# Graph attention on one core: a block's third gather ahead of its sums, a fourth load buffer, constants on GpSimd, x loaded later

## The chip, the core and the metric

The kernel runs on one core of one Trainium2 chip. The core has TensorE (PE in the profile; its weight loads stand apart as PEld), VectorE (DVE), ScalarE (ACT), GpSimd (POOL) and SyncE (SP), which run side by side, each through its own list of instructions in order, and wait for each other by semaphores. DMAs are issued from the queues of SP, ACT and POOL (SPq, ACTq, POOLq in the profile). The metric is the device time of one execution in microseconds (us), the median of the runs.

## What is computed

4096 nodes with 64 features, 50000 edges, 4 heads. Cut to what matters:

```python
x_proj[h] = x @ weight[h]
edge_scores[h] = leaky(sum(x_proj[h, src] * att_src[h]) + sum(x_proj[h, dst] * att_dst[h]))
for h in range(n_heads):
    for i in range(num_edges):
        output[h, dst[i]] += np.exp(edge_scores[h, i]) * x_proj[h, src[i]]
# and each output row is divided by the sum of its exps
```

`leaky` multiplies negative scores by 0.2. Edges come in any order; the sum over the edges of a destination is what costs.

## The kernel before, in words

**Sorting (two stages).** Every edge becomes one number that holds its source and destination. Stage 1 sorts 128 rows of 391 edges by source with compare-and-swap passes on DVE (class `Sorter`; `flip`, `half` and others, lines 187 to 252), while ACT counts with sign passes how many keys lie below each bound (`below`, line 263). The sorted rows go to memory (`store`, line 255), are fetched again by source group (`fetch`, line 306), and stage 2 sorts them by destination. Before stage 1, DVE and POOL build small constants (lines 81 to 159): signs per partition (`sj`, `sig`), offsets (`goff`, `off1`, `off2`, `boff`), bounds (`nb1`, `nb2`), partition numbers (`pF`) and selection masks (`m16`, `m8`, `sel1`, `sel2`). Stage 1 can start when the edges `eS` and `eD` have come from memory (lines 72 and 78).

**Tables.** Beside stage 1, PE and ACT make tables from `x` and `weight` (`tables`, lines 321 to 362): `xa` (features and source scores of each node, bf16) and `adb` (an identity and destination scores). `x` is 1 MB in `xf`; it and the weights `wS` are loaded by SP, directly behind the edges. PE's count for stage 1's bounds (`cnt_ps`, line 274) stands behind the tables in PE's list, and DVE reads it when stage 1 is sorted (line 276).

**Blocks.** The destinations are cut in 33 blocks of 125 (`ND`), the edges of a block in 16 groups of 128 (`NT`). For block b:

- `load(b)` (line 410, SP): 1 MB of source and destination numbers, spread to all partitions, into a buffer `bc`.
- `onehot(b)` (lines 438 and 439, DVE): three one-hot matrices `oh` for every group.
- `gather(b, c)` (lines 456 to 464), in three chunks c of 6, 6 and 4 groups: PE multiplies one-hots with the tables into a PSUM tile `ps` (two of these exist), ACT takes exponentials from it (`ex`, line 462) and copies it to `xs` (line 464). The next chunk but one needs that copy, since it uses the same `ps`.
- `weigh(b)` (lines 472 and 477, DVE): weights `wv` from `ex` of all three chunks, then `val` = weights times features from `xs` of all three chunks.
- `sums(b, k)` (lines 488 to 496, PE): k = -1 sums the weights, k = 0 and k = 1 multiply `val` with one-hots into the accumulator `acc`. After k = 1 ACT copies `acc` to `aT` (line 538).
- `project(b)` (line 542, PE) and, for every second block, `give` (lines 547 to 553: DVE divides into `res`, SP writes two blocks to the output).

The order on each engine is written out by hand in `run` (lines 502 to 524), which stands in the printed code below; each engine follows it in order. In the loop's body for block b, PE has: first chunk of b+1, project(b-1), sums(b,-1), second chunk of b+1, sums(b,0), third chunk of b+1, sums(b,1). DVE has weigh(b), onehot(b+2), and for even b the division. SP has the load, then for even b two output writes, which wait for DVE's division; a load also waits until the buffer that it fills has been read by `onehot`.

**Start of the block stage** (lines 614 to 622): POOL fetches windows of sorted edges, DVE unpacks them (`unpack`, lines 379 to 385), SP writes them to `gat_bins` (line 387), from which the loads read. Block 0 is spread on chip instead (`spread`).

The second version of the block stage, under `tc.If` at the end of the file, is for inputs with longer runs and isn't taken here.

Of the kernel before, what the change touches and what calls it, by code (L numbers as in the profile page):

```python
# [11 lines left out]
P = 128  # L12
# [4 lines left out]
OP = mybir.AluOpType  # L17
# [7 lines left out]
RL = RUN * L  # L25
W1 = 256
W2 = 128
BD = 125
# [9 lines left out]
def kernel(ctx: ExitStack, tc: tile.TileContext, x: bass.AP, edge_index: bass.AP,  # L38
                         weight: bass.AP, att_src: bass.AP, att_dst: bass.AP, out: bass.AP):
    nc = tc.nc  # L40
    V, S, G, T = nc.vector, nc.scalar, nc.gpsimd, nc.tensor
    N, Din = x.shape
# [3 lines left out]
    ND = -(-N // BD)  # L46
    NI = -(-ND // 8)
    SG = N // NR
# [32 lines left out]
    pidx = cst.tile([P, 1], I32)  # L81
# [6 lines left out]
    def bits(name, shift, mask):  # L88
        i = cst.tile([P, 1], I32, name=f"{name}_i")
        f = cst.tile([P, 1], F32, name=f"{name}_f")  # L90
        V.tensor_scalar(out=i[:], in0=pidx[:], scalar1=shift, scalar2=mask, op0=OP.logical_shift_right,
                        op1=OP.bitwise_and)
        V.tensor_copy(out=f[:], in_=i[:])
        return f


    sj = []
    for j in range(3):
        f = bits(f"b{j}", j, 1)
        V.tensor_scalar(out=f[:], in0=f[:], scalar1=-2.0, scalar2=1.0, op0=OP.mult, op1=OP.add)  # L100
        sj.append(f)
    sig = cst.tile([P, 1], F32)
    V.tensor_tensor(out=sig[:], in0=sj[0][:], in1=sj[1][:], op=OP.mult)
    V.tensor_tensor(out=sig[:], in0=sig[:], in1=sj[2][:], op=OP.mult)
    ioF = cst.tile([P, P], F32)
    V.tensor_copy(out=ioF[:], in_=io[:])
    nb1 = cst.tile([P, NR + 1], F32)
# [1 line left out]
    p8 = bits("p8", 3, 15)  # L109
# [11 lines left out]
    for i in range(3):  # L121
# [1 line left out]
        G.memset(eps[32 * i:32 * i + 1, :], float(term))  # L123
        left = left - term.astype(np.float32)
    goff = cst.tile([P, 1], F32)
    V.tensor_scalar(out=goff[:], in0=p8[:], scalar1=-float(SG * N), scalar2=None, op0=OP.mult)
    nb2 = cst.tile([P, ND + 1], F32)
    V.tensor_scalar(out=nb2[:], in0=ioF[:, 0:ND + 1], scalar1=-float(BD * SG), scalar2=-float(N * SG), op0=OP.mult,
                    op1=OP.max)
    V.tensor_scalar(out=nb2[:], in0=nb2[:], scalar1=0.5, scalar2=None, op0=OP.add)  # L130
    pF = cst.tile([P, 2], F32)
    V.tensor_copy(out=pF[:, 0:1], in_=pidx[:])
    V.tensor_scalar(out=pF[:, 1:2], in0=pF[:, 0:1], scalar1=float(P), scalar2=None, op0=OP.add)
    off1 = cst.tile([P, 2], F32)
    for i in range(2):
        V.tensor_scalar(out=off1[:, i:i + 1], in0=pm8[:], scalar1=float(RL), scalar2=float(8 * i * RL),
                        op0=OP.mult, op1=OP.add)
    off2 = cst.tile([P, 1], F32)
    V.tensor_scalar(out=off2[:], in0=pm16[:], scalar1=float(RL), scalar2=None, op0=OP.mult)
    boff = cst.tile([P, NI], F32)  # L140
    for i in range(NI):
        V.tensor_scalar(out=boff[:, i:i + 1], in0=p16[:], scalar1=-float(BD * SG), scalar2=-float(8 * i * BD * SG),
                        op0=OP.mult, op1=OP.add)
    m16 = cst.tile([P, 16], F32)
    G.tensor_scalar(out=m16[:], in0=ioF[:, 0:16], scalar1=p8[:, 0:1], scalar2=None, op0=OP.is_equal)
# [175 lines left out]
    def tables(pr, pps, pp1):  # L321

        S.copy(out=identb[:], in_=ident[:])
        xf = pr.tile([P, NB, Din], F32)
        nc.sync.dma_start(out=xf[:], in_=x.rearrange("(b p) d -> p b d", p=P))
        wS = pr.tile([Din, H, Dout], F32)
        nc.sync.dma_start(out=wS[:], in_=weight.rearrange("h c o -> c h o"))
        attbd = pr.tile([P, 2, 4], F32)
        G.memset(attbd[:], 0.0)
        for h in range(H):  # L330
            for k, a in enumerate((att_src, att_dst)):
                nc.gpsimd.dma_start(out=attbd[(h % 2) * 64:(h % 2) * 64 + 64, h // 2, 2 * k + h % 2:2 * k + h % 2 + 1],
                                    in_=a[h:h + 1, :].rearrange("a o -> o a"))
        G.memset(Wbd[:], 0.0)
        for h in range(H):
            hh = h % 2
            nc.gpsimd.dma_start(out=Wbd[hh * 64:hh * 64 + 64, h // 2, hh * 64:hh * 64 + 64], in_=weight[h, :, :])
        uv = pr.tile([Din, 2, H], F32)
        for i in range(2):
            ps = pps.tile([P, Din], F32, tag="pp")  # L340
            T.transpose(out=ps[:], in_=wS[:, 2 * i:2 * i + 2, :], identity=ident[0:Din, 0:Din])
            wT = pr.tile([P, Din], F32, name=f"wT{i}")
            S.copy(out=wT[:], in_=ps[:])
            ps2 = pps.tile([Din, 4], F32, tag="pp")
            T.matmul(out=ps2[:], lhsT=wT[:], rhs=attbd[:, i, :], start=True, stop=True)
            S.copy(out=uv[:, :, 2 * i:2 * i + 2], in_=av(ps2[:], 0, [2, 2], [1, 2]))
        S.copy(out=xa[:, :, 2 * H:XC], in_=xf[:])
        xT = pr.tile([Din, ND * BD + P - BD], F32)
        G.memset(xT[:, N:], 0.0)
        for q in range(NB // 4):  # L350
            ps = pps.tile([Din, 4, P], F32, tag="pp")
            for i in range(4):
                T.transpose(out=ps[:, i, :], in_=xf[:, 4 * q + i, :], identity=ident[:])
            S.copy(out=xT[:, 4 * q * P:4 * (q + 1) * P], in_=ps[:])
        for k, (n, step, to) in enumerate(((NB, P, xa[:, :, 0:2 * H]), (ND, BD, adb[:, :, P:AB]))):
            ps = pp1.tile([P, n, H], F32, name=f"at_ps{k}")
            for b in range(n):
                T.matmul(out=ps[:, b, :], lhsT=xT[:, b * step:b * step + P], rhs=uv[:, k, :], start=(b == 0), stop=True,  # L358
                         skip_group_check=True)
            S.copy(out=to[:, :, 0:H], in_=ps[:])  # L360
            S.mul(out=to[:, :, H:2 * H], in_=ps[:], mul=ALPHA)
        S.copy(out=adb[:, :, 0:P], in_=av(identb[:], 0, [0, ND], [1, P]))
# [32 lines left out]
    class Blocks:  # L395


        def __init__(self, ctx, sink):
            pool = lambda **kw: ctx.enter_context(tc.tile_pool(**kw))
            self.bcp = pool(name="bc", bufs=3)  # L400
            self.bp = pool(name="blk", bufs=2)
            self.psx = pool(name="ps_x", bufs=2, space=PSUM)
            self.psa = pool(name="ps_a", bufs=1, space=PSUM)
            self.sink = sink
            self.bc, self.oh, self.ex, self.xs, self.wv, self.val = ({} for _ in range(6))
# [96 lines left out]
        def run(self, also={}):  # L502
            for c in range(len(CH)):
                self.gather(0, c, V.tensor_copy if c == 1 else S.copy)
            self.onehot(1)
            for b in range(ND):
                self.load(b + 3)
                self.weigh(b, 2 if b == ND - 1 else 1)
                self.gather(b + 1, 0)
                self.onehot(b + 2)  # L510
                if b:
                    self.sink.project(b - 1)
                    if b % 2 == 0:
                        self.sink.give(b - 2, 2)
                self.sums(b, -1)
                self.gather(b + 1, 1)
                self.sums(b, 0)
                self.gather(b + 1, 2)
                self.sums(b, 1)
                if b in also:  # L520
                    also[b]()
            self.sink.project(ND - 1)
            n = 2 - ND % 2
            self.sink.give(ND - n, n)
# [89 lines left out]
    with ExitStack() as st:  # L614
        blocks = Blocks(st, Finish(st))
        win.unpack(0, nc.sync, nc.scalar)
        for b in range(1, 3):
            blocks.load(b)
        for i in range(1, 4):
            win.unpack(i, nc.sync, nc.sync)  # L620
        blocks.spread(0, win.tb[:, 0])
        blocks.run({i - 3: lambda i=i: win.unpack(i, nc.sync, nc.sync) for i in range(4, NI)})
# [3 lines left out]
    with tc.If((n1 > W1) | (n2 > W2)):  # L626
        with tc.tile_pool(name="all", bufs=1) as al:
            total = al.tile([P, ND, AW], F32)
            V.memset(total[:], 0.0)
            with tc.For_i(0, n1, W1):  # L630
                at1 = advance(al, ws1, we1, W1, 1)
                with tc.tile_pool(name="sort3", bufs=1) as so3, tc.tile_pool(name="pp3", bufs=1, space=PSUM) as pp3:
                    group(so3, pp3, at1[:])
                    longest(so3, pp3, ws2, we2, 1)
                m2 = room(1, L)
                with tc.For_i(0, m2, W2):
                    with ExitStack() as st:
                        win = Windows(st.enter_context(tc.tile_pool(name="win", bufs=1)), advance(al, ws2, we2, W2, 2)[:])
                        for i in range(NI):
                            win.unpack(i, nc.sync, nc.scalar)  # L640
                        blocks = Blocks(st, Total(total))
                        for b in range(3):
                            blocks.load(b)
                        blocks.onehot(0)
                        blocks.run()
# [39 lines left out]
```

## Time and profile before

| | us |
|---|---|
| median of 3 runs (lowest, highest) | 319.4 (318.13, 319.46) |
| the profiled execution | 319.96 |
| its span, first to last instruction | 318.1 |
| busy in the span: PE, DVE, ACT, POOL | 209.2, 273.6, 180.6, 19.0 |

The span is cut as follows by the places where an engine takes up the next stage: stage 1 from 5.79 to 70.83 us, stage 2 from 79.10 to 117.04, the block loop's steady part from 141.59 (block 1's `val`) to 301.98 (block 31's `val`). Shares of busy time over the whole span are averages over these stages; what a change in the loop can bring is read in the loop. A timeline row gives the start and the length of an instruction, and in brackets how long its engine stood idle before it and what ended that. Neighbouring instructions on one engine may overlap by some hundredths of a us.

### The profile page before, as it was taken

How to read it: one execution, taken by the hardware profiler on the slowest of the kernel's cores; microseconds unless marked ns; L12 is line 12 of the kernel's file. 1: busy time of each engine (PE TensorE's matmuls, PEld its weight loads, DVE VectorE, ACT ScalarE, POOL GpSimd, SP SyncE). 2: the span in 40 equal slices, each digit the busy share in tenths (PEclk: the TensorE clock that was granted, in tenths of full speed). 3: DMA queues.
4: the chain of work that ended last, by engine and by line, in shares of the span. 5: the costliest groups of instructions: out<-in, count | busy, mean ns of one | idle time of the engine just before them, and what ended most of it. 6: DMA issues, size and time to landing. Idle time of an engine off the chain costs nothing. (4 is left out here: it accounts for less than half of the span.)

```text
span 318.1 us, 8412 instructions
## 1 busy us (share of the span) xinstructions
PE 209.2 (66%) x3534; PEld 193.3 (61%) x3534; DVE 273.6 (86%) x519; ACT 180.6 (57%) x351; POOL 19.0 (6%) x46
## 2 busy tenths in 40 slices
PE   0039999000000008499999989999999999999981
PEld 0027999000000003398989888988888889888970
DVE  7999999993999986889998899899978998899860
ACT  2984001300999400557768767767767677777740
POOL 6800000002000005000000000000000000000000
PEclk9999555555555555979999999999999999999997
DMA  7200000002000002963844865586458556755312
GB/s 201 50 1 0 2 0 0 1 0 66 1 0 0 1 33 51 302 255 102 293 165 193 285 225 163 217 292 223 163 220 279 183 179 258 279 181 187 118 36 55
DMA packets 13070, 41.80 MB, mean 131 GB/s; under 512 B 3088, under 2 KB 8272, under 8 KB 8928
## 3 DMA queue, kind: packets, MB, share of 16 engines
q1 hardware_dynamic: 11944, 40.09, 36.4%
q0 software_dynamic: 704, 0.66, 0.9%
q8 instruction: 30, 0.49, 0.6%
q10 hardware_dynamic: 376, 0.43, 0.4%
q14 instruction: 16, 0.13, 0.1%
HBM read 36.13 MB, written 5.05 MB: 129 GB/s over the span
## 5 line engine op out<-in xcount | busy, mean ns | idle before, releaser
L464 ACT CAST xs<-ps 128x1200 bf16<-128x1200 f32 (+1 forms) x98 | 102.0, 1041 | 0.0
L477 DVE TENSOR_TENSOR val<-xs,wv 128x4096 bf16<-128x4096 bf16 (+1 forms) x34 | 75.7, 2229 | 9.6 <-ACT xs L464 7.8
L496 PE MATMUL acc<-xs,val 128*128 128x125 bf16 x1056 | 70.0, 220 | 9.9 <-DVE val L477 9.0
L456 PE MATMUL ps<-xa,oh 128*128 128x72 bf16 x528 | 73.9, 197 | 3.6 <-DVE oh L438 2.9
L460 PE MATMUL ps<-adb,oh 128*128 128x136 bf16 x528 | 76.0, 225 | 0.0
L458 PE MATMUL ps<-xa,oh 128*128 128x72 bf16 x528 | 73.4, 198 | 1.3 <-DVE oh L439 1.1
L496 PEld LDWEIGHTS <-val 128*128 128x128 bf16 x1056 | 60.5, 99 | 14.8 <-DVE val L477 14.8
L456 PEld LDWEIGHTS <-oh 128*128 128x128 bf16 x528 | 52.2, 99 | 3.5 <-DVE oh L438 3.5
L462 ACT ACTIVATE ex<-ps 128x96 bf16<-128x96 f32 (+1 forms) x99 | 24.2, 245 | 52.1 <-PE ps L460 51.8
L458 PEld LDWEIGHTS <-oh 128*128 128x128 bf16 x528 | 51.9, 98 | 2.9 <-DVE oh L439 2.6
L460 PEld LDWEIGHTS <-oh 128*128 128x128 bf16 x528 | 52.0, 98 | 0.0
L438 DVE TENSOR_SCALAR oh<-bc,pF 128x4096 bf16<-128x4096 bf16 (+2 forms) x35 | 42.8, 1222 | 6.5 <-DMA bc<-gat_bins 5.8
L201 DVE TENSOR_TENSOR sA<-sB 128x256 f32<-128x256 f32 (+2 forms) x108 | 39.7, 409 | 1.9
L201 DVE TENSOR_TENSOR sB<-sA 128x256 f32<-128x256 f32 (+2 forms) x100 | 36.8, 409 | 1.7
L263 ACT ACTIVATE junk<-kr,nb 128x512 f32<-128x512 f32 x33 | 23.8, 722 | 21.9 <-DVE kr L314 20.9
L274 PE MATMUL cnt_ps<-sgn,sel 128*128 128x17 f32 (+1 forms) x6 | 1.7, 390 | 52.2 <-ACT sgn L266 52.2
L274 PEld LDWEIGHTS cnt_ps<-sgn,sel 128*128 128x128 f32 x6 | 1.4, 318 | 52.3 <-issue 52.3
L358 PEld LDWEIGHTS at_ps<-uv,xT 64*128 64x128 f32 x130 | 25.7, 307 | 0.2 <-issue 0.2
L358 PE MATMUL at_ps<-uv,xT 64*128 64x4 f32 x130 | 25.8, 335 | 0.0
L439 DVE TENSOR_SCALAR oh<-bc,pF 128x2048 bf16<-128x2048 bf16 (+2 forms) x35 | 25.1, 717 | 0.0
L542 PE MATMUL pf<-Wbd,aT 128*125 128x128 f32 x132 | 21.9, 288 | 1.7 <-ACT aT L538 0.9
L542 PEld LDWEIGHTS pf<-Wbd,aT 128*125 128x125 f32 x132 | 17.0, 187 | 3.8 <-issue 1.9
(125 smaller groups left out, 200.6 us busy)
## 6 DMA issues: line engine op xcount, KB each, us to landing
bc<-gat_bins SPq DMA_DIRECT2D x32, 1024.0 KB, 9.1
out_dram<-res SPq DMA_DIRECT2D x32, 125.0 KB
gat_sorted<-sA SPq DMA_DIRECT2D x2, 256.0 KB
eS<-in_edge_index_dram SPq DMA_DIRECT2D x1, 390.0 KB
eD<-in_edge_index_dram ACTq DMA_DIRECT2D x1, 390.0 KB
gat_bins<-tb SPq DMA_DIRECT2D x9, 32.0 KB
out_dram<-res SPq DMA_DIRECT2D x1, 96.0 KB, 3.5
win<-gat_sorted,wi POOLq DMA_INDIRECT x5, 2.6
```

Of the source, the lines that this page charges most:

```text
L201: V.tensor_tensor(out=av(d[:], o, [2 * h, n], [1, h]), in0=av(s[:], 0, [2 * h, n], [1, h]), in1=av(s[:], h, [2 * h, n], [1, h]), op=op)
L358: T.matmul(out=ps[:, b, :], lhsT=xT[:, b * step:b * step + P], rhs=uv[:, k, :], start=(b == 0), stop=True, skip_group_check=True)
L438: V.tensor_scalar(out=oh[:, 0:2, e], in0=bc[:, :, e], scalar1=pF[:, 0:1], scalar2=None, op0=OP.is_equal)
L439: V.tensor_scalar(out=oh[:, 2, e], in0=bc[:, 1, e], scalar1=pF[:, 1:2], scalar2=None, op0=OP.is_equal)
L456: T.matmul(out=ps[:, i, P:P + XC], lhsT=oh[:, 1, e], rhs=xa[:, 2 * t, :], start=(i % 2 == 0), stop=False, skip_group_check=True)
L458: T.matmul(out=ps[:, i, P:P + XC], lhsT=oh[:, 2, e], rhs=xa[:, 2 * t + 1, :], start=False, stop=False, skip_group_check=True)
L460: T.matmul(out=ps[:, i, 0:S0], lhsT=oh[:, 0, e], rhs=adb[:, b, :], start=False, stop=True, skip_group_check=True)
L462: S.activation(out=av(ex[:], 2 * t0, [2, n], [2 * NT, 2 * H], [1, 2]), in_=av(ps[:], P, [PW, n], [1, 2 * H], [0, 2]), func=ACTF.Exp)
L464: copy(out=xs[:, t0:t0 + n, 0:P + XC], in_=ps[:, 0:n, 0:P + XC])
L477: V.tensor_tensor(out=av(val[:], h * Dout, [Dout, n], [C, NT], [1, Din]), in0=av(xs[:], S0, [0, n], [XW, NT], [1, Din]), in1=av(wv[:], h * ...
L496: T.matmul(out=self.acc[:, k * BD:(k + 1) * BD], lhsT=val[:, t, k * P:(k + 1) * P], rhs=xs[:, t, 0:BD], start=False, stop=(t == NT - 1), s ...
L542: T.matmul(out=self.pf[0:BD, b % 2, k * P:(k + 1) * P], lhsT=self.aT[:, b % 2, k * BD:(k + 1) * BD], rhs=Wbd[:, k, :], start=(b % 2 == 0 a ...
```

## The change

It has five parts. In `run`, the third chunk of block b+1 stands ahead of `sums(b, 0)` instead of behind it. The pool of `bc` has four buffers instead of three, and loads are issued one block earlier (b+4 in place of b+3, three in place of two before the loop). 25 small constant operations go from DVE to POOL. `x` and `weight` are loaded from ACT's queue; in ACT's list that stands behind the 16 sign passes of stage 1. In the version that isn't taken, loads are one more as well. The diff, with constants of the same kind left out:

```diff
         V.tensor_scalar(out=i[:], in0=pidx[:], scalar1=shift, scalar2=mask, op0=OP.logical_shift_right,
                         op1=OP.bitwise_and)
-        V.tensor_copy(out=f[:], in_=i[:])
+        G.tensor_copy(out=f[:], in_=i[:])
...
-        V.tensor_scalar(out=f[:], in0=f[:], scalar1=-2.0, scalar2=1.0, op0=OP.mult, op1=OP.add)
+        G.tensor_scalar(out=f[:], in0=f[:], scalar1=-2.0, scalar2=1.0, op0=OP.mult, op1=OP.add)
...
-    V.tensor_tensor(out=sig[:], in0=sig[:], in1=sj[2][:], op=OP.mult)
+    G.tensor_tensor(out=sig[:], in0=sig[:], in1=sj[2][:], op=OP.mult)
...
-        V.tensor_scalar(out=boff[:, i:i + 1], in0=p16[:], scalar1=-float(BD * SG), scalar2=-float(8 * i * BD * SG),
+        G.tensor_scalar(out=boff[:, i:i + 1], in0=p16[:], scalar1=-float(BD * SG), scalar2=-float(8 * i * BD * SG),
                         op0=OP.mult, op1=OP.add)
...
-        nc.sync.dma_start(out=xf[:], in_=x.rearrange("(b p) d -> p b d", p=P))
+        nc.scalar.dma_start(out=xf[:], in_=x.rearrange("(b p) d -> p b d", p=P))
         wS = pr.tile([Din, H, Dout], F32)
-        nc.sync.dma_start(out=wS[:], in_=weight.rearrange("h c o -> c h o"))
+        nc.scalar.dma_start(out=wS[:], in_=weight.rearrange("h c o -> c h o"))
...
-            self.bcp = pool(name="bc", bufs=3)
+            self.bcp = pool(name="bc", bufs=4)
...
-                self.load(b + 3)
+                self.load(b + 4)
...
                 self.gather(b + 1, 1)
+                self.gather(b + 1, 2)
                 self.sums(b, 0)
-                self.gather(b + 1, 2)
                 self.sums(b, 1)
...
-        for b in range(1, 3):
+        for b in range(1, 4):
             blocks.load(b)
```

How it stands on PE in the loop's body for block 1, before (`ps_1211` is block 2's second chunk, `ps_1248` its third; `acc_1193` and `val_1157` are block 1's; rows of a chunk or a sum that read alike are left out):

```order
L488 MATMUL acc_1193<-eps_115,one_116 128x4
L491 MATMUL acc_1193<-wv_1155,xs_1033 128x4
...
L460 MATMUL ps_1211<-adb_158,oh_1055 128x136
L496 MATMUL acc_1193<-xs_1033,val_1157 128x125
...
L456 MATMUL ps_1248<-xa_157,oh_1055 128x72
L460 MATMUL ps_1248<-adb_158,oh_1055 128x136
```

And after (the tiles' numbers are two higher up to the second chunk; the third is `ps_1234`):

```order
L488 MATMUL acc_1195<-eps_115,one_116 128x4
L491 MATMUL acc_1195<-wv_1157,xs_1035 128x4
...
L460 MATMUL ps_1213<-adb_158,oh_1057 128x136
...
L460 MATMUL ps_1234<-adb_158,oh_1057 128x136
L496 MATMUL acc_1195<-xs_1035,val_1159 128x125
```

The third chunk has moved from behind the first sixteen matmuls on `val` to in front of them; both sums of `val` now stand together.

SP's list from the program's start into the loop, as a difference:

```order
 L78 DMA eS<-in_edge_index_dram 80x2
-L325 DMA xf<-in_x_dram 128x32x64
-L327 DMA wS<-in_weight_dram 64x4x64
 L255 DMA gat_sorted<-sA 128x512 x2
 L297 TENSOR_LOAD most x2
 L387 DMA gat_bins<-tb 8x16x128
-L410 DMA bc<-gat_bins 128x4096 x2
+L410 DMA bc<-gat_bins 128x4096 x3
 L387 DMA gat_bins<-tb 8x16x128 x6
```

The loads of x and the weights have left SP, and a third load stands ahead of the six writes of unpacked windows; behind that the pattern of two output writes and two loads is the same as before, with each load for the block after the one that it was for.

POOL's list at the program's start, as a difference:

```order
 masks.py:199 AFFINE_SELECT ident<-ident 128x128
+L93 CAST b_f<-b_i 128x1
+L100 TENSOR_SCALAR b_f<-b_f 128x1
...
+L103 TENSOR_TENSOR sig<-b_f 128x1
+L104 TENSOR_TENSOR sig<-sig,b_f 128x1
...
+L126 TENSOR_SCALAR goff<-p_f 128x1
+L128 TENSOR_SCALAR nb_126<-ioF 128x34
...
+L142 TENSOR_SCALAR boff<-p_f 128x1 x5
 L145 TENSOR_SCALAR m_143<-ioF,p_f 128x16
```

The constants that left DVE now stand in POOL's list ahead of the masks, so that the masks, POOL's DMAs for the attention weights and `Wbd` come later.

## Rows read from the trace of the kernel before

**Rows 1.** Stretches: start:end, length; PE, PEld, DVE, ACT, POOL busy; clock; DMA.

```profile
5.79:70.83 65.04, 34.74 (x172) 31.94 (x172) 62.05 (x167) 24.66 (x52) 8.38 (x20) 0.69 0.07 15
141.59:301.98 160.39, 149.58 (x3046) 142.19 (x3043) 143.97 (x155) 115.82 (x212) 0.00 (x0) 1.00 0.59 208
```

**Rows 2.** Waits, loop from 141.59 to 301.98: total us, times, longest.

```profile
PE acc L496 <- DVE val L477: 8.4, 15, 0.6
DVE val L477 <- ACT xs L464: 7.3, 15, 0.5
DVE oh L438 <- DMA bc<-gat_bins: 5.8, 14, 0.9
```

**Rows 3.** DVE's timeline, a pair of blocks: start, length, line, [idle before <-releaser].

```profile
206.00 2.29 DVE L477 TENSOR_TENSOR val<-xs,wv 128x4096 bf16<-128x4096 bf16 x1
208.21 1.28 DVE L438 TENSOR_SCALAR oh<-bc,pF 128x4096 bf16<-128x4096 bf16 x1
...
210.19 0.23 DVE L472 TENSOR_TENSOR wv<-ex 128x128 bf16<-128x128 bf16 x1
210.91 2.29 DVE L477 TENSOR_TENSOR val<-xs,wv 128x4096 bf16<-128x4096 bf16 x1 [0.49 <-ACT xs L464]
213.44 1.28 DVE L438 TENSOR_SCALAR oh<-bc,pF 128x4096 bf16<-128x4096 bf16 x1 [0.24 <-DMA bc<-gat_bins]
...
215.59 0.69 DVE L549 TENSOR_TENSOR res<-pf,inv 125x512 f32<-125x512 f32 x1
...
216.51 2.29 DVE L477 TENSOR_TENSOR val<-xs,wv 128x4096 bf16<-128x4096 bf16 x1
```

**Rows 4.** PE's timeline, same pair.

```profile
208.34 1.05 PE L496 MATMUL acc<-xs,val 128*128 128x125 bf16 x16 [0.57 <-DVE val L477]
...
212.97 0.22 PE L460 MATMUL ps<-adb,oh 128*128 128x136 bf16 x1
```

**Rows 5.** ACT's timeline, same pair: copies of the first and the third chunk.

```profile
206.00 1.15 ACT L464 CAST xs<-ps 128x1200 bf16<-128x1200 f32 x1
...
210.05 0.82 ACT L464 CAST xs<-ps 128x800 bf16<-128x800 f32 x1
```

**Rows 6.** SP's timeline, same pair, and issues by line (KB each, median us to landing).

```profile
206.51 0.83 SPq L410 DMA_DIRECT2D bc<-gat_bins  x2
...
bc<-gat_bins SPq DMA_DIRECT2D x24, 1024.0 KB, 9.1
```

**Rows 7.** Timelines of DVE and PE at the loop's start and end.

```profile
140.87 0.22 DVE L472 TENSOR_TENSOR wv<-ex 128x128 bf16<-128x128 bf16 x1 [0.99 <-ACT ex L462]
...
306.18 0.22 DVE L472 TENSOR_TENSOR wv<-ex 128x128 bf16<-128x128 bf16 x1 [1.91 <-ACT ex L462]
...
308.21 2.15 PE L496 MATMUL acc<-xs,val 128*128 128x125 bf16 x32
```

**Rows 8.** Timeline of the program's start, POOL and DVE.

```profile
3.79 0.30 POOL L147 TENSOR_SCALAR m<-ioF,p_f 128x8 f32<-128x8 f32 x1
...
5.79 0.51 DVE L597 TENSOR_SCALAR sli<-eS 128x391 int32<-128x391 int32 x1 [0.32 <-DMA eS<-in_edge_index_dram]
```

**Rows 9.** Timeline of the unpacking, one DVE operation with and without POOL beside it.

```profile
125.56 0.46 DVE L383 TENSOR_SCALAR t<-kb 128x128 int32<-128x128 int32 x1
...
126.81 0.22 DVE L383 TENSOR_SCALAR t<-kb 128x128 int32<-128x128 int32 x1
...
125.02 0.94 POOL L306 DMA_INDIRECT win<-gat_sorted,wi  x1 [0.30 <-issue]
```

**Rows 10.** Timelines of PE, ACT and DVE around the tables.

```profile
11.62 0.34 PE L341 MATMUL ps<-ident,wS 64*128 64x64 f32 x1 [11.62 <-DMA wS<-in_weight_dram]
...
19.30 0.29 ACT L323 CAST identb<-ident 128x128 bf16<-128x128 f32 x1
...
54.22 1.03 PE L274 MATMUL cnt_ps<-sgn,sel 128*128 128x17 f32 x4
...
70.83 0.17 DVE L276 TENSOR_SCALAR cnt<-cnt_ps 128x17 f32<-128x17 f32 x1
```

More of the change, by code (lines that the diff above doesn't have):

```diff
@@ L99 @@
         f = bits(f"b{j}", j, 1)
-        V.tensor_scalar(out=f[:], in0=f[:], scalar1=-2.0, scalar2=1.0, op0=OP.mult, op1=OP.add)
+        G.tensor_scalar(out=f[:], in0=f[:], scalar1=-2.0, scalar2=1.0, op0=OP.mult, op1=OP.add)
         sj.append(f)
     sig = cst.tile([P, 1], F32)
-    V.tensor_tensor(out=sig[:], in0=sj[0][:], in1=sj[1][:], op=OP.mult)
-    V.tensor_tensor(out=sig[:], in0=sig[:], in1=sj[2][:], op=OP.mult)
+    G.tensor_tensor(out=sig[:], in0=sj[0][:], in1=sj[1][:], op=OP.mult)
+    G.tensor_tensor(out=sig[:], in0=sig[:], in1=sj[2][:], op=OP.mult)
     ioF = cst.tile([P, P], F32)
@@ L125 @@
     goff = cst.tile([P, 1], F32)
-    V.tensor_scalar(out=goff[:], in0=p8[:], scalar1=-float(SG * N), scalar2=None, op0=OP.mult)
+    G.tensor_scalar(out=goff[:], in0=p8[:], scalar1=-float(SG * N), scalar2=None, op0=OP.mult)
     nb2 = cst.tile([P, ND + 1], F32)
-    V.tensor_scalar(out=nb2[:], in0=ioF[:, 0:ND + 1], scalar1=-float(BD * SG), scalar2=-float(N * SG), op0=OP.mult,
+    G.tensor_scalar(out=nb2[:], in0=ioF[:, 0:ND + 1], scalar1=-float(BD * SG), scalar2=-float(N * SG), op0=OP.mult,
                     op1=OP.max)
-    V.tensor_scalar(out=nb2[:], in0=nb2[:], scalar1=0.5, scalar2=None, op0=OP.add)
+    G.tensor_scalar(out=nb2[:], in0=nb2[:], scalar1=0.5, scalar2=None, op0=OP.add)
     pF = cst.tile([P, 2], F32)
-    V.tensor_copy(out=pF[:, 0:1], in_=pidx[:])
-    V.tensor_scalar(out=pF[:, 1:2], in0=pF[:, 0:1], scalar1=float(P), scalar2=None, op0=OP.add)
+    G.tensor_copy(out=pF[:, 0:1], in_=pidx[:])
+    G.tensor_scalar(out=pF[:, 1:2], in0=pF[:, 0:1], scalar1=float(P), scalar2=None, op0=OP.add)
     off1 = cst.tile([P, 2], F32)
     for i in range(2):
-        V.tensor_scalar(out=off1[:, i:i + 1], in0=pm8[:], scalar1=float(RL), scalar2=float(8 * i * RL),
+        G.tensor_scalar(out=off1[:, i:i + 1], in0=pm8[:], scalar1=float(RL), scalar2=float(8 * i * RL),
                         op0=OP.mult, op1=OP.add)
     off2 = cst.tile([P, 1], F32)
-    V.tensor_scalar(out=off2[:], in0=pm16[:], scalar1=float(RL), scalar2=None, op0=OP.mult)
+    G.tensor_scalar(out=off2[:], in0=pm16[:], scalar1=float(RL), scalar2=None, op0=OP.mult)
     boff = cst.tile([P, NI], F32)
     for i in range(NI):
-        V.tensor_scalar(out=boff[:, i:i + 1], in0=p16[:], scalar1=-float(BD * SG), scalar2=-float(8 * i * BD * SG),
+        G.tensor_scalar(out=boff[:, i:i + 1], in0=p16[:], scalar1=-float(BD * SG), scalar2=-float(8 * i * BD * SG),
                         op0=OP.mult, op1=OP.add)
@@ L641 @@
                         blocks = Blocks(st, Total(total))
-                        for b in range(3):
+                        for b in range(4):
                             blocks.load(b)
```

## The prediction

> **What bounds the kernel now.** I read the stretches of the stages first, then the waits of the longest stage, then the engines' timelines for one pair of blocks. Sorting is DVE's: in stage 1 it is busy 62.05 of 65.04 us, with PE and ACT half idle [rows 1]. The steady block loop is half of the span: 160.39 us for 30 blocks (15 pairs, 10.69 us each), with DVE busy 143.97, PE 149.58 and ACT 115.82 [rows 1]. PE's number is the largest, but its matmuls overlap, so I looked for who waits for whom. DVE waits 7.3 us in 15 places for ACT's `xs` and 5.8 us in 14 places for a load `bc`; PE waits 8.4 us for DVE's `val` [rows 2]. So DVE sets the pace, and it is held up from outside for 13.1 us.
>
> One pair shows how. From `val` at 206.00 to the `val` two blocks on at 216.51 are 10.51 us, with two waits, 0.49 (`xs`) and 0.24 (`bc`) [rows 3]. Without them DVE's own work is 9.78 us a pair; from the sums over the loop it is (160.39 - 13.1) / 15 = 9.82. PE's own work for a block, from the start of `sums(b,0)` at 208.34 to the end of the next block's second chunk (last matmul starts at 212.97, the next could start some 0.06 later), is 4.69 us without a wait between [rows 4], so 9.4 a pair. PE has 0.4 us a pair to spare once DVE runs unhindered.
>
> **The third chunk ahead of the sums.** The wait for `xs` is a circle: `val(b)` ends at 206.00 + 2.29 = 208.29, `sums(b,0)` starts at 208.34 [rows 4], the third chunk follows, ACT copies it from 210.05 to 210.87 [rows 5], and only then can `val(b+1)` start, at 210.91 [rows 3]. After the change the third chunk doesn't wait for `val(b)`. PE stands idle from 208.34 - 0.57 = 207.77 [rows 4] and can make it there. Its `ps` must have been copied: the first chunk's copy ends at 206.00 + 1.15 = 207.15 [rows 5], 0.6 us earlier. The chunk is at most 0.66 us long (from 208.34 plus the sums' 1.05 to ACT's copy at 210.05), so it ends by 208.4, and the sums start 0.1 later at worst. ACT then has two copies in a row, 1.15 + 0.82 [rows 5], and two exponentials, for which I allow 0.4: done by 207.77 + 2.37 = 210.14. DVE would want `xs` at 210.91 - 0.49 = 210.42. It is there, with 0.3 us left. Gain: the whole 7.3 us less the one at 141.59 (it belongs to the start), so 14 x 0.49 = **6.8 us**.
>
> What is late next? `sums(b,1)` now ends 1.8 us after `val(b)`, and the next block's first chunk wants the one-hots, which DVE ends 210.15 - 208.29 = 1.9 us after `val(b)` (the next row starts at 210.19) [rows 3]. A new wait on PE of some 0.2 us in one block of a pair; queued behind it are the projection and the weights' sums, and for those DVE doesn't wait. It comes out of PE's 0.4 us. ACT does what it did, in the same order.
>
> **The fourth buffer.** SP issues loads in pairs, behind the two output writes that wait for the division `res`: at 206.51 in the pair shown [rows 6]. The first of the pair is wanted at 213.20 and came at 213.44, 6.9 us after its issue [rows 3]; the median from issue to landing is 9.1 us [rows 6]. The buffers were free long before; what is late is the issue, held by SP's order. With loads for one block later at the same place of the list, the same two issues serve blocks that DVE reads some five us later, so the first would have 12 us and the second 17 against 7 to 9.1. Nothing of the 14 waits is left: **5.8 us**. DMA moves the same bytes at a mean share of 0.59 [rows 1], 0.64 at the new pace. Before the loop, the third load moves ahead of six window writes; they are read only by the load for block 8, so I cost it at nothing.
>
> **Loop's start and end.** At 140.87 `wv` waited 0.99 and the `val` behind it 0.49, both for block 1's third chunk [rows 2, 7]. ACT must finish the second chunk's copy first, so not all goes: **0.8** of 1.5. At the end `wv` waits 1.91 [rows 7], but the last sums at 308.21 [rows 7] follow PE's sums of the block before and the copy of its `acc`, which stay: I take **0.5**, between 0 and 1.9.
>
> **Constants on GpSimd.** DVE's first work on edges waits 0.32 us for them [rows 8]: the 25 operations were over before the edges came. Taking them away gains nothing unless the edges come sooner. On POOL one costs about 0.30 [rows 8], so 25 x 0.30 = 7.5 us, and the masks and POOL's DMAs move back by some 6. Nobody waits for POOL there until the tables. But POOL's small operations, over by 5.8 before, now reach to some 13 us, 5 to 6 us of them beside stage 1, in which every us of DVE counts. Does DVE slow down beside POOL? One row speaks for it: the same 128x128 operation took 0.46 us while POOL worked and 0.22 when it had ended [rows 9]. That is 0.24 for one operation. Bounds: nothing, and 6 us if DVE stood still for each of them. I take **0.8 lost**, near the small end, because most of these operations touch one element per partition. The Trainium skill speaks against this edit (SBUF — State Buffer, "Who interferes with whom"): a DVE instruction with two SBUF inputs contends with a GpSimd instruction that reads SBUF, and one of them blocks fully. The sort's compare passes are of that kind; the doubled row agrees in direction, and no row here shows a compare pass beside such a POOL operation.
>
> **x from ACT's queue.** The edges stand ahead of x in SP's queue, so they gain little by its absence: **0**, with 0.5 either way. The tables start later. PE had the weights at 11.62 us [rows 10], so load and weights take at most 11.6 us from issue. ACT now issues at 19.3 [rows 10], so tables start by 30.9 where the second part of them started at about 19.6: 11.3 us later. They cover that: PE's count behind them ends at 55.25, and DVE reads it at 70.83 [rows 10], 15.6 later. If the cover were gone, every us beyond 15.6 would count.
>
> **The sum.** 6.8 + 5.8 + 0.8 + 0.5 - 0.8 = 13.1 us off the profiled execution of 319.96 (span 318.1 and 1.9 around it), so 306.9. That execution stands 0.6 above the median of 319.4; against the median: **306.3 us**.
>
> **The rivals.**
> 1. *POOL stops DVE in stage 1.* For it: the doubled row [rows 9], and DVE is the sort's bound [rows 1]. Against: the operations are tiny. 6 us lost in place of 0.8: 311.5. The skill's rule above, taken literally, is this case.
> 2. *PE takes over.* Its 9.4 plus the new 0.2 are close to DVE's 9.8; if `ps` comes free later than I think, or the third chunk's copy is late by more than 0.3, a pair takes 10.1: 15 x 0.3 = 4.5 lost, 310.8. Deeper, with the pair back at 10.7, only the start and end are left and the time is within 0.5% of before (about what a measurement can tell from no change): 318.5.
> 3. *The fourth buffer doesn't help,* because loads are limited by how fast memory delivers and not by their issue. For it: 9.1 us of a 10.5 us pair is loading. Against: a mean share of 0.59. The 5.8 stay: 312.1.
> 4. *Slower than before.* The third chunk now stands in front of the sums in PE's order. If ACT's copy of the first chunk frees `ps` late, PE waits there and the sums, the copy of `acc` and the next block with it. Before, a block took 5.35 us; PE's 4.69 exceeds that once it waits over 0.66, which needs the copy to end over 1.2 us later than at 207.15. At 1.5 us late a block takes 5.6: 30 x 0.25 = 7.5 us more, 327. Nothing in the rows makes ACT that late.
>
> **How the numbers follow.** Forecast 0.64 (its own range 303.5 to 308.5); rival 1: 0.12; rival 2: 0.11 at 310.8 and 0.04 within 0.5%; rival 3: 0.05; rival 4: 0.04. Faster by over 0.5%: 0.64 + 0.12 + 0.11 + 0.05 = 0.92; within: 0.04; slower: 0.04. The range takes in rivals 1, 2 and 3 above, and below the forecast half a us for earlier edges, the 0.8 not lost, and 1 to 2 us at the loop's ends: 303.0 to 312.5.
>
> **What the profile after would show.** Right: a loop pair of 9.8 us, no wait of DVE for `xs` or `bc`, some waits of PE for one-hots, stage 1 (from the first key operation to the read of the count) 65 to 66 us, `cnt_ps` by 67 us, DVE still starting on edges at 5.5 to 5.8. Wrong: compare passes longer than before while POOL builds constants (rival 1), DVE waiting for ACT every block (rival 2), waits for `bc` still there (rival 3), PE waiting for ACT at the third chunk (rival 4), or a first key operation well before 5 us, which would mean that x did hold back the edges.

## The result, and the profile after

The changed kernel takes 304.56 us (median of 4 runs, 304.01 to 305.14) against 319.43 for the kernel before beside it: a ratio of 0.9537, 95% interval 0.9498 to 0.9577. It is faster by 14.9 us. Forecast were 306.3, and 303.0 to 312.5 as the range. The profiled execution takes 304.22 us, its span is 301.83 against 318.09.

The same two stretches as in [rows 1], stage 1 and the loop's steady part, with the same columns:

```profile
5.69:70.62 64.93, 34.49 (x172) 31.68 (x172) 61.95 (x168) 24.79 (x53) 14.90 (x34) 0.76 0.10 19
140.17:286.62 146.45, 145.32 (x3058) 142.20 (x3056) 141.44 (x154) 114.92 (x211) 0.00 (x0) 1.00 0.64 224
```

Stage 1 is as long as before (64.93 against 65.04), though POOL now works 14.90 us in it instead of 8.38. The loop has gone from 160.39 to 146.45 us. The waits in it, against [rows 2] (left out is ACT's wait for `ps`; ACT has time to spare):

```profile
...
ACT aT L538 <- PE acc L496: 5.6, 15, 0.6
PEld L496 <- DVE val L477: 3.3, 14, 0.2
DVE val L477 <- ACT xs L464: 0.5, 1, 0.5
```

DVE's 14 waits for loads are gone, and of its waits for `xs` one is left, at the loop's first block. What stays of waits between DVE and PE is small and on PE's side: its weight loads wait for `val`, 3.3 us in 14 places. DVE's timeline of a pair, against [rows 3]:

```profile
194.04 2.29 DVE L477 TENSOR_TENSOR val<-xs,wv 128x4096 bf16<-128x4096 bf16 x1
196.25 1.28 DVE L438 TENSOR_SCALAR oh<-bc,pF 128x4096 bf16<-128x4096 bf16 x1
...
198.11 0.19 DVE L547 RECIPROCAL inv<-aT 125x8 f32<-125x8 f32 x1
198.40 0.69 DVE L549 TENSOR_TENSOR res<-pf,inv 125x512 f32<-125x512 f32 x1
199.00 0.22 DVE L472 TENSOR_TENSOR wv<-ex 128x128 bf16<-128x128 bf16 x1
199.32 2.29 DVE L477 TENSOR_TENSOR val<-xs,wv 128x4096 bf16<-128x4096 bf16 x1
201.53 1.28 DVE L438 TENSOR_SCALAR oh<-bc,pF 128x4096 bf16<-128x4096 bf16 x1
202.73 0.75 DVE L439 TENSOR_SCALAR oh<-bc,pF 128x2048 bf16<-128x2048 bf16 x1
203.39 0.22 DVE L472 TENSOR_TENSOR wv<-ex 128x128 bf16<-128x128 bf16 x1
203.74 2.29 DVE L477 TENSOR_TENSOR val<-xs,wv 128x4096 bf16<-128x4096 bf16 x1
```

No row has a bracket: a pair takes 203.74 - 194.04 = 9.70 us of DVE's own work, and pairs in the middle of the loop agree with that within 0.01. ACT's copy of the third chunk, which set `val` before ([rows 5]), now ends at 203.27, 0.47 ahead of the `val` that reads it:

```profile
202.43 0.84 ACT L464 CAST xs<-ps 128x800 bf16<-128x800 f32 x1
```

SP's list around the pair, and its loads by line, against [rows 6]: the loads are issued at the same place, behind the writes, and take as long from issue to landing (9.0 us at the median), but nobody waits for them.

```profile
199.12 0.68 SPq L553 DMA_DIRECT2D out_dram<-res  x2
199.84 0.83 SPq L410 DMA_DIRECT2D bc<-gat_bins  x2
...
bc<-gat_bins SPq DMA_DIRECT2D x32, 1024.0 KB, 9.0
```

Where the span's 16.26 us went, stretch by stretch (before, after): up to block 0's `val` 135.73, 135.11; from there to block 1's 5.86, 5.06; the loop 160.39, 146.45; from block 31's `val` to the end 16.11, 15.20. That is 0.62 + 0.80 + 13.94 + 0.90.

### The profile page after: what moved, and what is told of

It reads as the page before. It is cut to its first block, busy times and chain, and to the rows that moved or that the text cites. A ratio compares the mean times of both kernels' runs of the same rounds, so it can differ in the third digit from the quotient of the medians.

```text
span 301.8 us, 8411 instructions
## 1 busy us (share of the span) xinstructions
PE 203.1 (67%) x3534; PEld 192.0 (64%) x3534; DVE 267.4 (89%) x494; ACT 179.7 (60%) x352; POOL 26.1 (9%) x71
## 5 line engine op out<-in xcount | busy, mean ns | idle before, releaser
L456 PE MATMUL ps<-xa,oh 128*128 128x72 bf16 x528 | 72.5, 197 | 3.6 <-DVE oh L438 2.9
L460 PE MATMUL ps<-adb,oh 128*128 128x136 bf16 x528 | 73.5, 226 | 0.0
L458 PE MATMUL ps<-xa,oh 128*128 128x72 bf16 x528 | 71.7, 198 | 0.6 <-DVE oh L439 0.5
L496 PE MATMUL acc<-xs,val 128*128 128x125 bf16 x1056 | 63.7, 218 | 1.2
L496 PEld LDWEIGHTS <-val 128*128 128x128 bf16 x1056 | 59.1, 98 | 3.5 <-DVE val L477 3.5
L462 ACT ACTIVATE ex<-ps 128x96 bf16<-128x96 f32 (+1 forms) x99 | 25.0, 253 | 30.1 <-PE ps L460 30.1
L263 ACT ACTIVATE junk<-kr,nb 128x512 f32<-128x512 f32 x33 | 23.8, 722 | 13.6 <-DVE kr L314 12.5
L341 PE MATMUL ps<-ident,wS 64*128 64x64 f32 x2 | 0.7, 350 | 27.7 <-DMA wS<-in_weight_dram 27.7
```

Of the source, the lines that this page charges most:

```text
L263: S.activation(out=junk[:], in_=v, func=ACTF.Sign, bias=nbnd[:, b:b + 1], scale=1.0, accum_out=sgn[:, b:b + 1])
L456: T.matmul(out=ps[:, i, P:P + XC], lhsT=oh[:, 1, e], rhs=xa[:, 2 * t, :], start=(i % 2 == 0), stop=False, skip_group_check=True)
L458: T.matmul(out=ps[:, i, P:P + XC], lhsT=oh[:, 2, e], rhs=xa[:, 2 * t + 1, :], start=False, stop=False, skip_group_check=True)
L460: T.matmul(out=ps[:, i, 0:S0], lhsT=oh[:, 0, e], rhs=adb[:, b, :], start=False, stop=True, skip_group_check=True)
L462: S.activation(out=av(ex[:], 2 * t0, [2, n], [2 * NT, 2 * H], [1, 2]), in_=av(ps[:], P, [PW, n], [1, 2 * H], [0, 2]), func=ACTF.Exp)
L496: T.matmul(out=self.acc[:, k * BD:(k + 1) * BD], lhsT=val[:, t, k * P:(k + 1) * P], rhs=xs[:, t, 0:BD], start=False, stop=(t == NT - 1), s ...
```

## The experiments

The loop's numbers stand together here; "loop" is from block 1's `val` to block 31's, "pair" the mean of 12 pairs in its middle (block 5's `val` to block 29's), both read from the profiled run. The kernel before took 319.18, 319.07 and 320.15 us beside the three groups (e1 to e4; a2, e7, e8 and e9; e5 and e10), and each ratio is to the kernel before of its own group; it comes from all runs, and so is not quite the quotient of the medians.

| kernel | us | ratio to before (interval) | loop | pair |
|---|---|---|---|---|
| before | 319.43 | 1 | 160.39 | 10.70 |
| third chunk alone (e1) | 318.09 | 0.9978 (0.9959 to 0.9997) | 159.65 | 10.66 |
| fourth buffer alone (e2) | 313.16 | 0.9823 (0.9793 to 0.9853) | 153.28 | 10.19 |
| start alone (e3) | 318.20 | 0.9975 (0.9954 to 0.9995) | 159.42 | 10.66 |
| three buffers, loads first (e4) | 313.54 | 0.9832 (0.9801 to 0.9864) | 153.28 | 10.19 |
| loop's parts alone (e9) | 304.52 | 0.9551 (0.9526 to 0.9577) | 146.84 | 9.70 |
| after, repeated (a2) | 304.41 | 0.9559 (0.9535 to 0.9584) | 146.59 | 9.70 |
| after + 30 GpSimd operations (e5) | 305.98 | 0.9573 (0.9543 to 0.9603) | 146.55 | 9.70 |
| after + 8 matmuls per block (e7) | 306.09 | 0.9595 (0.9570 to 0.9620) | 148.57 | 9.79 |
| after, `wv` between the one-hots (e8) | 312.08 | 0.9776 (0.9754 to 0.9798) | 152.51 | 10.08 |
| after, division between (e10) | 299.32 | 0.9363 (0.9333 to 0.9393) | 140.85 | 9.35 |

### e1: the third chunk alone

```diff
                 self.gather(b + 1, 1)
+                self.gather(b + 1, 2)
                 self.sums(b, 0)
-                self.gather(b + 1, 2)
                 self.sums(b, 1)
```

> The kernel before with the third chunk ahead of the sums, and nothing else of the change. Theory: the two waits of DVE sit in one circle. The first load of a pair is issued behind the output writes, right after the division ends (206.28 - 10.51 = 205.77 in the pair shown), and lands 7.7 us later, whatever DVE does between; DVE gets there 0.49 earlier and waits 0.49 longer for the load (0.24 becomes some 0.7 to 0.8). The pair stays at 10.7 us and only the loop's two ends gain: 318 us, 14 waits for loads worth 12 to 13 us in place of 5.8, no wait for xs. Rival (the waits are independent and add): the 6.8 us and the ends are gained here as well, 311 us, with the waits for loads still at 5.8.

318.09 us, 1.1 less than the kernel before beside it, where the term for this edit was 6.8 us. The waits for `xs` did go; those for loads took their place. Waits of DVE from 141 to 290 us, and its timeline over one pair:

```profile
DVE oh L438 <- DMA bc<-gat_bins: 11.3, 13, 1.3
...
DVE val L477 <- ACT xs L464: 0.5, 1, 0.5
```

```profile
201.06 1.29 DVE L438 TENSOR_SCALAR oh<-bc,pF 128x4096 bf16<-128x4096 bf16 x1 [1.06 <-DMA bc<-gat_bins]
...
203.20 0.69 DVE L549 TENSOR_TENSOR res<-pf,inv 125x512 f32<-125x512 f32 x1
...
211.61 1.29 DVE L438 TENSOR_SCALAR oh<-bc,pF 128x4096 bf16<-128x4096 bf16 x1 [0.76 <-DMA bc<-gat_bins]
```

SP's rows of the same pair:

```profile
203.92 0.68 SPq L553 DMA_DIRECT2D out_dram<-res  x2
204.64 0.83 SPq L410 DMA_DIRECT2D bc<-gat_bins  x2
...
214.48 0.68 SPq L553 DMA_DIRECT2D out_dram<-res  x2
215.20 0.84 SPq L410 DMA_DIRECT2D bc<-gat_bins  x2
```

This is a circle: the load is issued at 204.64, its one-hot starts at 211.61, the division behind that one-hot lets SP write and issue the next load at 215.20. That is 6.97 + 3.59 = 10.56 us, and DVE's other work fits inside it, whether or not it waits 0.49 for `xs`. (It is not equally long in every pair: the twelve pairs of e1 take 10.50 to 11.08 us.) So the wait for `xs` in the kernel before lay inside the load's circle, and to take it out alone moves it into the wait for the load.

### e2 and e4: the fourth buffer alone, and the loads' place without the buffer

e2 is the kernel before with four buffers and loads for b + 4. e4 keeps three buffers, and puts the two loads ahead of the output writes in SP's list, so that each pair of loads that follows a pair of writes is for blocks one later, as in e2:

```diff
-                self.load(b + 3)
+                if b < 3:
+                    self.load(b + 3)
+                    if b == 2:
+                        self.load(6)
+                elif b % 2 == 0:
+                    self.load(b + 3)
+                    self.load(b + 4)
```

> The kernel before with the fourth load buffer and loads one block earlier, and nothing else. Theory: the waits for loads go, and each was worth its idle time plus the 0.08 us by which DVE otherwise starts an instruction before the last has ended: 5.8 + 14 x 0.08 = 7.0 us; the wait for xs stays at 0.49 a pair. 312.4 us, pair 10.20. Rival (memory delivers too slowly, so the waits move rather than go): 317 to 319, waits for loads still there.

> The kernel before, with three buffers, but with the two loads of a pair put ahead of the two output writes in SP's list, so that each pair of loads that follows a pair of writes is for blocks one later. Theory (the place in SP's list was the cause, not the number of buffers): the first load of a pair finds its buffer free and the second waits one block for it, with two and a half blocks to spare; the waits for loads go as with four buffers, 312.4 us, the same as the fourth buffer alone. Rival (a buffer too few): the second load of each pair is late now, waits for loads stay at 5 us or more, 318 us or slower.

313.16 and 313.54 us, the same loop to a hundredth. Neither has a wait for a load; both keep those for `xs` (the row is the same in e2 and in e4, over the same stretch as above):

```profile
DVE val L477 <- ACT xs L464: 7.3, 15, 0.5
```

e4 has as many buffers as the kernel before. So the loads were late because they stood behind the writes in SP's list, as the prediction read [rows 6], not because buffers or memory were short. In e4's rows the two issues take 4.0 us together, since SP now waits there for a buffer to come free (they end at 206.97, just behind the one-hots of that buffer, which DVE ends at 205.84 + 0.75 = 206.59):

```profile
202.23 0.68 SPq L559 DMA_DIRECT2D out_dram<-res  x2
202.96 4.01 SPq L410 DMA_DIRECT2D bc<-gat_bins  x2
```

Alone, the two edits take 0.7 and 7.1 us off the loop; together (e9) 13.6. The rest, 5.7 us, exists only when both are done.

### e3 and e9: the start alone, and the loop's parts alone

e3 is the changed kernel with the loop of before; e9 is the kernel before with the changed order and the fourth buffer, without the constants on POOL and x on ACT's queue.

> The kernel before with the constants on GpSimd and x loaded from ACT's queue, and the block loop as before. Theory: the edges' landing sets the start and GpSimd gives way to the compare passes, so stage 1 from the first key operation to the read of the count stays within 0.2 us of 65.0; first key operation at 5.7: 319.2 us, no change. Rival (a GpSimd operation that reads SBUF stops a compare pass): up to 5 us more in stage 1, 324. Rival (x held the edges back): first key operation 0.5 us or more earlier, 318.5 or less.

> The third chunk ahead of the sums and the fourth load buffer together; the constants stay on VectorE and x and the weights stay on SyncE's queue. Theory (moving constants and x is worth nothing; the 1 us that they gained alone came from waits for loads that fell out otherwise and from run to run variation before the first block): within 0.5 us of the changed kernel, 304.1 to 305.1, with a pair of 9.70 us. Rival (the move is worth a us by itself, as it showed alone): 305.6 or more.

e9 took 304.52, the changed kernel beside it 304.41: constants and x are worth nothing that these runs can tell. By itself (e3) the move gained 1.0 us, with an interval of 0.2 to 1.5. Its trace puts 0.6 us before block 0's `val`, at 135.10; but kernels whose start was that of before have it at 134.76 (e2), 135.01 (e1), 135.33 (e4) and 135.73 (before), so that much comes and goes from run to run. Another 1.0 lies in the loop, where 11 waits for loads take 4.9 us in place of 14 with 5.8. Why loads landed a little sooner there was not settled; where no wait for a load is left, it can't matter.

### a2 and e7: the changed kernel again, and eight more matmuls per block

```diff
+                for _ in range(8):
+                    T.matmul(out=self.acc[:, 2 * BD:AW], lhsT=one[:], rhs=nil[:], start=False, stop=False,
+                             skip_group_check=True)
                 for t in range(NT):
```

> The changed kernel once more, beside the variants of it that run with it. 304.6 us, as in its first runs. A pair of blocks in the loop takes 9.70 us from one weighting (val) to the next but one.

> The changed kernel with 8 more small matmuls of zeros per block ahead of the weights' sums, at some 0.028 us each (0.22 us per block, 0.45 per pair). Theory (VectorE's own work sets the pair of 9.70 us and TensorE has some 0.25 us of it to spare): a pair of about 9.9 us, 15 x 0.2 = 3 us slower than the changed kernel, 306.5 to 308.5. Rival A (TensorE has more than 0.45 us to spare): 304.6, no change. Rival B (TensorE is the bound already): 15 x 0.45 = 6.8 us slower, 311.

306.09 us, 1.7 more than a2. The eight took 0.20 us, less than the 0.22 expected (PE's timeline, from the start of the first to the next line's start):

```profile
197.40 0.34 PE L491 MATMUL acc<-nil,one 128*128 128x4 bf16 x8
197.60 0.56 PE L494 MATMUL acc<-wv,xs 128*128 128x4 bf16 x16
```

So 0.40 a pair was added, and most pairs grew by 0.06, to 9.76; one took 10.12. The wait of DVE for `xs` is back, at 0.2 us a pair (its first 0.13 costs nothing, since `val` starts that much behind the end of `wv` without a wait too, as the next section shows):

```profile
DVE val L477 <- ACT xs L464: 3.5, 15, 0.5
```

PE thus had 0.34 us a pair to spare in the changed kernel: its own work is 9.36 a pair (the prediction had 9.4), DVE's 9.70. The theory's 3 us and its 306.5 or more were too much because this room was put at 0.25; rival A, no change, did not come either.

### e8 and e10: DVE's order in a block

In the timeline of after, `val` starts 0.35 us behind the start of a `wv` that is 0.22 long, so 0.13 after its end, while operations that don't read their neighbour's result start 0.08 before its end (201.53 + 1.28 = 202.81, the next at 202.73). e8 puts `wv` and the reciprocal between the two one-hot operations of every block; e10 does so only with the division's parts. DVE's order in a block with a division:

```
after: val, one-hot 1, one-hot 2, reciprocal, division, wv, val
e8:    val, one-hot 1, wv, reciprocal, one-hot 2, division, val
e10:   val, one-hot 1, reciprocal, one-hot 2, wv, division, val
```

In a block without one, e8 has `wv` between the one-hots, and e10 leaves the order as it was.

> The changed kernel with VectorE's order in a block changed: the next block's small weight product wv goes between the two one-hot operations, and the reciprocal too, so that val doesn't follow directly behind the wv that it reads. Theory (VectorE's own work sets the pair; 0.1 us of latency before each val and 0.1 before the division go): a pair of 9.4 us on VectorE, which TensorE's 9.45 then sets: 9.45 to 9.6, 1.5 to 4 us faster than the changed kernel, 300.6 to 303.1. Rival A (TensorE sets the pair already): 304.6. Rival B (wv now waits for ScalarE's exponentials and one-hots come later for TensorE): 306 or more.

> The changed kernel with VectorE's order in a block changed once more: in a block with a division the order is first one-hot operation, reciprocal, second one-hot operation, wv, division, val; in a block without one it stays first, second, wv, val. So wv is asked for only 0.8 us earlier than in the changed kernel, and behind ScalarE's last exponential (which ended 0.36 us before that point there). Theory (latency between an operation and the next that reads it is worth 0.38 us a pair on VectorE, and TensorE has room for 0.39 by the run with eight more matmuls): a pair of 9.3 to 9.5 us, 3 to 6 us faster than the changed kernel, 298.5 to 301.5. Rival A (TensorE and ScalarE don't follow, the wait for xs in the block without a division grows by as much): a pair of 9.65 to 9.7, 303.5 to 304.6. Rival B (wv waits for ScalarE as it did between the one-hots): 306 or more.

e8 took 312.08 us, 7.7 more: rival B. `wv` needs ScalarE's exponentials of all three chunks, and asked for them too early once a pair (DVE's timeline, then its waits from 145 to 290 us):

```profile
201.37 0.23 DVE L478 TENSOR_TENSOR wv<-ex 128x128 bf16<-128x128 bf16 x1 [0.72 <-ACT ex L469]
...
DVE wv L478 <- ACT ex L469: 10.6, 14, 1.3
```

e10 took 299.32 us, 0.9363 of before (0.9333 to 0.9393), the fastest of all; against a2 the loop is 5.7 us shorter. DVE's timeline over a pair:

```profile
201.56 2.29 DVE L486 TENSOR_TENSOR val<-xs,wv 128x4096 bf16<-128x4096 bf16 x1 [0.21 <-ACT xs L471]
203.77 1.28 DVE L442 TENSOR_SCALAR oh<-bc,pF 128x4096 bf16<-128x4096 bf16 x1
204.97 0.20 DVE L564 RECIPROCAL inv<-aT 125x8 f32<-125x8 f32 x1
205.08 0.70 DVE L433 TENSOR_SCALAR oh<-bc,pF 128x2048 bf16<-128x2048 bf16 x1
205.70 0.22 DVE L478 TENSOR_TENSOR wv<-ex 128x128 bf16<-128x128 bf16 x1
205.83 0.69 DVE L569 TENSOR_TENSOR res<-pf,inv 125x512 f32<-125x512 f32 x1
206.43 2.28 DVE L486 TENSOR_TENSOR val<-xs,wv 128x4096 bf16<-128x4096 bf16 x1
```

From `val` to `val` in the block with the division it is 4.87 us, where it was 5.28. The reciprocal costs 0.11 and `wv` 0.13, as the next operation doesn't read them. The pair is 9.35 to 9.37, but for the first of the twelve, and that is what e7 gave as PE's own work. DVE's wait for `xs` of some 0.2 is back in the other block, as in e7. The loop's columns agree, with PE busy for all of it; alone they would say little, as PE reads 145.32 of 146.45 in the changed kernel, with 0.34 a pair to spare.

```profile
140.01:280.84 140.83, 140.83 (x3039) 140.37 (x3036) 137.49 (x154) 114.72 (x211) 0.00 (x0) 1.00 0.66 237
```

So with e10 the loop seems to have passed from DVE to PE; no run with more work for either engine was made on e10 to test it.

### e5: thirty more GpSimd operations beside stage 1

```diff
         G.memset(xT[:, N:], 0.0)
+        idle = pr.tile([P, P], F32)
+        for _ in range(30):
+            G.tensor_scalar(out=idle[:], in0=ioF[:], scalar1=p8[:, 0:1], scalar2=None, op0=OP.is_equal)
```

> The changed kernel with 30 more GpSimd operations on 128x128 f32 beside the sort's first stage, their result unread (0.3 to 0.6 us each, 9 to 18 us of GpSimd, all of it beside VectorE's compare passes). Theory (GpSimd gives way to VectorE, not VectorE to GpSimd): stage 1 from the first key operation to the count's read stays 64.9 to 65.5 us, 304.4 to 305.2 in all, and the added operations take longer than 0.30 us. Rival (VectorE stops for a GpSimd operation that reads SBUF): at 0.3 us for each 9 us more, at 0.59 us for each 17.7 us more, 313 to 322.

305.98 us, 0.9573 of the kernel before, where a2 was 0.9559: not told apart by these intervals. Its trace shows a small price all the same, more than the theory allowed (stage 1 up to 65.5 us). Stage 1 lasts from 5.72 to 72.17, 66.45 us against 64.93, so 1.5 more, 0.05 for each. POOL's row of the added operations, and two compare passes of DVE beside them, then the same two passes in the changed kernel:

```profile
L352 POOL TENSOR_SCALAR idle<-ioF,p_f x30: 613/752/1212, 22.4 to 46.7; 128x128 f32<-128x128 f32 x30
...
31.04 0.81 DVE L201 TENSOR_TENSOR sB<-sA 128x256 f32<-128x256 f32 x2
```

```profile
30.33 0.76 DVE L201 TENSOR_TENSOR sB<-sA 128x256 f32<-128x256 f32 x2
```

Two passes grew from 0.76 to 0.81 us, and an operation on POOL, of the same kind and shape as one that took 0.59 at 5.23 us in the kernel before, took 0.75 (the median). Both give a little, and POOL more.

## Why the prediction was right, and where it was off

**The third chunk and the fourth buffer: right together.** Their sum was 12.6 us for the loop, and 13.94 came. The mechanisms are shown: e1's waits for `xs` go with the order, e2's for loads with the place in the list (e4). But 6.8 and 5.8 as prices of single edits were wrong: the sum took two waits on one engine as additive, and alone they are worth 0.7 and 7.1 in the loop. What the runs show is two circles: the load's (10.56 us in the pair shown, 10.66 in e1's mean) and the one through `xs` (10.19, e2's pair) ran side by side, and a pair takes the longer. Rival 3 (the fourth buffer doesn't help) is excluded by e2.

**DVE's own work was mis-sized, 9.78 to 9.82 for 9.70.** The step that failed is the subtraction of the waits from the pair. A wait costs its idle time and also the 0.08 us by which an operation that doesn't wait starts before its neighbour's end: in [rows 3] the one-hot at 208.21 follows `val` by 2.21 us, the one that waited 0.24 follows it by 2.53. For 14 waits that is 14 x 0.08 = 1.1 us, which with the 12.6 makes 13.7 of the 13.94. That 0.49 was the right price for `xs` is luck. `val` starts 0.13 behind the end of `wv` even without a wait, so only 0.36 of the 0.49 could go. But `wv` was late too, by a wait for ACT's exponentials too short to be listed: in the kernel before it starts 0.79 behind the second one-hot (the row here, then 210.19 in [rows 3]), in the changed one 0.66 (202.73 to 203.39). Together that is the 0.49 between e2's pair and the changed kernel's.

```profile
209.40 0.75 DVE L439 TENSOR_SCALAR oh<-bc,pF 128x2048 bf16<-128x2048 bf16 x1
```

**The new wait on PE did not come where it was put.** It was to wait 0.2 us for one-hots; instead its weight loads wait 0.2 for `val` once a pair. The size was right, and PE's room, put at 0.4, is 0.34 (e7). Rival 2 was near: with 0.06 us a pair beyond that room e7 already shows DVE's wait for `xs` again. Rival 4 (PE waits for ACT's copy) is not in the trace: PE has no wait for ACT among the loop's waits.

**Start and end of the loop.** 0.8 was forecast for the start and 0.80 measured; but repeats of the changed loop have 4.77 (a2) and 5.41 (e9) in that place, where the profiled run had 5.06, so part of the agreement is luck. The end gained 0.90 in place of 0.5: the wait of `wv` there fell from 1.91 [rows 7] to 0.98, and e1 has the same end, 15.19.

```profile
289.90 0.23 DVE L472 TENSOR_TENSOR wv<-ex 128x128 bf16<-128x128 bf16 x1 [0.98 <-ACT ex L462]
```

**Constants: 0.8 lost was wrong, 0.1 was.** POOL's constants reach into stage 1 as forecast, up to about 12.8 us, but most passes beside them keep their length (0.36 us, for example those at 7.93 before and 7.68 after). Two grow by 0.05 each, beside the 128x128 masks: the single one at 11.71 (0.36 in the kernel before) and the two at 12.42 (0.68 for 0.63), and so in every trace with the constants on POOL. POOL's masks stretch more: the one of [rows 8] from 0.30 to 0.58. In the whole time the 0.1 can't be seen (e9).

```profile
7.68 0.36 DVE L191 TENSOR_TENSOR sA<-key 128x196 f32<-128x196 f32 x1
...
9.86 0.58 POOL L147 TENSOR_SCALAR m<-ioF,p_f 128x8 f32<-128x8 f32 x1
...
11.71 0.41 DVE L191 TENSOR_TENSOR sA<-sB 128x192 f32<-128x192 f32 x1
```

The Trainium skill (SBUF — State Buffer, "Who interferes with whom") says that a DVE instruction with two SBUF inputs contends with a GpSimd instruction that reads SBUF, and calls the shared port pair an exclusive lock; taken literally, with one of the two standing still, that gives rival 1. Its direction holds, as both do slow down in e5; for these operations the full stop does not: at the 0.59 us of an undisturbed one, DVE would have lost 30 x 0.59 = 17.7 us, and it lost 1.5. The doubled row [rows 9] was no sign of it either: that operation has one tensor input, not two, and what POOL does beside it is a fetch by DMA; and in the changed kernel the same operation at 122.89 takes 0.22 with POOL's fetch from 122.41 to 123.36 beside it, so what doubled it before stays open.

**x from ACT's queue: right.** PE has the weights at 27.68 instead of 11.62 [rows 10], and the count behind the tables starts at 62.46 instead of 54.22, still 8 us ahead of DVE's read at 70.62; the first key operation starts at 5.69, within the half us allowed either way. In the seven traces with x on ACT's queue and the constants on POOL it starts at 5.63 to 5.75, in the five with both where they were at 5.66 to 6.28. So one of the two may have held back the edges by a few tenths in some executions; the runs don't tell which, nor tell it from chance.

```profile
5.69 0.36 DVE L597 TENSOR_SCALAR sli<-eS 128x391 int32<-128x391 int32 x1 [3.47 <-DMA eS<-in_edge_index_dram]
...
27.68 0.34 PE L341 MATMUL ps<-ident,wS 64*128 64x64 f32 x1 [27.68 <-DMA wS<-in_weight_dram]
...
62.46 1.03 PE L274 MATMUL cnt_ps<-sgn,sel 128*128 128x17 f32 x4
```

**The sum.** Of the 2.7 us between 306.9 and 304.22, 1.3 lie in the loop, 0.4 at its end, 1.4 before block 0's `val` (the 0.8 that does not show there, and 0.6 within what that stretch does from run to run), and 0.5 go the other way around the span (2.4 instead of 1.9).

## What to carry to other kernels

Before waits on one engine are added up, ask which circle each belongs to: the longest circle sets the pace, and a wait inside a shorter one is worth nothing until the longer is cut. A load that comes late may be a matter of where it stands in its queue's list; compare issue, landing and use before buying a buffer. When an engine works without waits, look at neighbours of which one reads the other's result: putting an independent operation between them took 5.7 us off the loop here (e10), but only where its inputs were ready in time.

## What the hardware showed that was not expected

A small DVE operation whose result the next one reads costs 0.29 to 0.35 us from start to start (reciprocal 198.11 to 198.40, `wv` 203.39 to 203.74), and 0.11 to 0.13 where the next one doesn't read it (e10, 204.97 to 205.08 and 205.70 to 205.83). The Trainium skill says of VectorE that the next operation does not start until the pipe has emptied, that leaving out semaphores doesn't avoid it, and that a next operation that is not held starts earlier (VectorE: DVE Perf Modes, "The DRAIN you can't avoid"). These rows agree with the last, and show that the order of operations avoids a good part of the gap. And GpSimd beside two-input passes of DVE cost DVE 0.05 us for an operation of 0.75 us (e5), not a stop.
